# Splitting plain weight blocks by DMA: a casting transfer for the rounded half, a negative on ACT and an adding transfer for the rest

## Chip, cores and metric

The kernel runs on one core of a Trainium2 chip. Its engines are PE (matrix products; PEld is its weight load), DVE and ACT (elementwise work), POOL (a slower elementwise engine) and SP (which here only issues DMA transfers). The metric is the device time of one execution in microseconds. The kernel before took 1035.16 us in the median of three timed runs (1034.41 to 1039.77).

## What is computed

One step of a one-layer decoder on 560 tokens (16 meta tokens, 512 of a prompt, 8 x 4 of running sequences), in float32:

```python
x = x + 0.5 * swiglu(rmsnorm(x, g_ff1), w_ff1_gate, w_ff1_up, w_ff1_down)
mix, new_state = mixer(rmsnorm(x, g_mix), W, l, st)   # 4 mLSTM heads beside an RG-LRU
x = x + mix
x = x + 0.5 * swiglu(rmsnorm(x, g_ff2), w_ff2_gate, w_ff2_up, w_ff2_down)
y = rmsnorm(x, g_final)

def swiglu(x, w_gate, w_up, w_down):
    return (jax.nn.silu(x @ w_gate) * (x @ w_up)) @ w_down
```

The model width is 1024 (8 blocks of 128 rows), that of the FFNs 2816 (22 blocks). The mixer multiplies its input by `w_in` (queries, keys, values, gates, RG-LRU inputs), runs the recurrences, and multiplies the result by `w_out`.

## The kernel before

**Products.** PE multiplies operands in the type fp32r, a rounded float32. To keep float32's accuracy every operand is split into a rounded half `hi` (a copy into an fp32r tile) and a rest `lo` (the operand minus `hi`, again fp32r), and each product is made in three passes: `w_hi * x_hi`, `w_hi * x_lo`, `w_lo * x_hi` (`split_mm`, line 286).

**Weights.** They come as a list, `units`, of blocks of 128 x 512 in the order of their use. There are two kinds. *Plain* units are blocks of a weight matrix as it stands: 64 of `w_down`, 50 of `w_in`, 24 of gate and up, 16 of `w_out`, 154 in all. The others belong to 45 *sets of seven products* (Strassen's, in Winograd's form, `product7`, line 397): a set loads four quarters (`w11`, `w21`, `w22`, `w12`) and DVE makes four sums of them (`quarter_sum`, line 236), and seven units are used.

Whenever a product takes its unit (`next_w`), `run_ahead` brings four steps forward, each by its own lead in units, `AHEAD = 8, 6, 5, 4`:

- `load`: SP issues a DMA from HBM into a tile `raw` (line 223 for a plain unit, 226 for a quarter);
- `sums`: the sums of quarters, on DVE (line 236);
- `split_hi`: ACT copies `raw` (or a sum) into the fp32r tile `whi` (line 256);
- `split_lo`: DVE subtracts `whi` from `raw` and writes `wlo` (line 261).

The three kinds of tile have six buffers each (`wp`, `bufs=6`, tags `raw`, `hi`, `lo`). A load waits until the tile that it takes over is free: a `raw` is free when ACT and DVE have read it, a `whi` or `wlo` when PE has.

**Stages.** FFN 1 (from 0 to about 375 us) begins with plain units, while DVE and ACT normalise x, then alternates sets of seven products with plain units of `w_down`. The mixer (about 375 to 690 us) uses the 50 plain units of `w_in` and the 16 of `w_out`. FFN 2 (690 to about 1000 us) is built as FFN 1, and the last norm ends the kernel.

**Order.** On PE, ACT and DVE the program's own order of writing holds (tables such as `PLAN` and `FF1`). POOL and SP are placed by a scheduler. POOL's work before the change: the sums of squares of the norms (`square`, line 366, seven adds of which the last is DVE's; in FFN 1 `start_add`, line 665), the mixer's constants (lines 794 to 834, among them the masked RG-LRU weights `wrg`, `wrgh`, `wrgl`), for the gates' product `pgate` two casts that pack `lo` columns beside `hi` columns (line 873; PE uses them at 876), copies of keys and values that PE transposes, and sums for denominators. `mean` (line 379) is the product `psn` that takes `acc`, the finished sum of squares, to the mean; the scale made from it (line 383) is needed by every result of the mixer's first products.

Of the kernel before, what the change touches and what calls it, by code (L numbers as in the profile page):

```python
# [11 lines left out]
P = 128  # L12
KD = 8            # 1024 / 128
KF = 22           # 2816 / 128
T = 560           # 16 meta + 512 prompt + 8 x 4 sample tokens
C16 = 16
TQ = T - C16      # tokens whose outputs are needed
NP = 528
Q = 280           # half of the tokens
AHEAD = 8, 6, 5, 4          # how far loads, sums and both steps of the split run ahead of the products  # L20
MANUAL = {mybir.EngineType.PE, mybir.EngineType.Activation, mybir.EngineType.DVE}
TCUT = 272        # where the last row blocks are cut
DED = 7           # row blocks of h with a place of their own
PLAIN = 4, 3      # row blocks of h from plain products, in both FFNs
FT = 15           # where the last row blocks of h are cut for w_down
TAIL = 5          # row blocks of x that FFN 2 ends with
# [5 lines left out]
# the mixer, in the order of its steps (see there)  # L32
# [35 lines left out]
IN = [t for t in PLAN if t == "g" or t[0] in "kqvoxy" and t[1].isdigit()]       # row blocks of w_in  # L68
OUT = (4, 5, 6, 7, 0, 1, 2, 3)                                   # rows of w_out
# [5 lines left out]
# the beginnings of both FFNs, in the order of their steps (see `ffn`)  # L75
# [10 lines left out]
# columns of the constant array  # L86
G1, GM, G2, GF = 0, 8, 16, 24
CW = 32           # [ct, 4]
# [6 lines left out]
CS = 72           # [ct, b, 3]  # L95
H0 = 168          # [ct, b]
N0 = 200          # [h, b]
NCONST = 232

# Products of h with w_down (see `ffn`): of its second part, and under them the first part is made in quarters,  # L100
# with their sums; then the seven products of every pair of row blocks, and between them some of the others.
# [15 lines left out]
# The seven products: weights, right side, bank, and whether they open it. After one, what its bank holds goes  # L117
# into a quarter of the result.
# [6 lines left out]
# packed columns of the causal weights of one head, by block of keys  # L125
WO = (0, 512, 912, 1184, 1328, 1344)
WTOT = 1376
T0 = (16, 128, 256, 384, 512)      # first query of each block of keys
KROWS = (128, 128, 128, 128, 16, 32)

# columns of the output array of small states
# [5 lines left out]
def hymba_step(ctx, tc, xT, wgu1, wdn1, win, wout, wgu2, wdn2, consts, small, c0t, wrg,  # L137
# [6 lines left out]
    wp = ctx.enter_context(tc.tile_pool(name="wp", bufs=6))  # L144
# [4 lines left out]
    # ---------------------------------------------------------------- weights  # L149
    # Products take their weights in the order of this list, 512 columns at a time: blocks of w, or  # L150
    # quarters and sums of quarters of [gate, up] (see ups7). Loads and splits run ahead of them.
# [19 lines left out]
    def blocks(ff):  # L171
        """Row blocks of h: the plain ones, those that go through w_down by seven products, the others, and these
        in two parts."""
        a, b = PLAIN[ff], PLAIN[ff] + 8
        return (0, a), (a, b), {"d": (b, KF), "e": (b, FT), "t": (FT, KF)}
# [29 lines left out]
    loaded, ready = {}, {}  # L205
    state = {"use": 0}

    def raw_tile():
        return wp.tile([P, 512], F32, tag="raw", name="raw")

    def hl_tile():
        return (wp.tile([P, 512], F32R, tag="hi", name="whi"), wp.tile([P, 512], F32R, tag="lo", name="wlo"))
# [6 lines left out]
    def load(i):  # L219
        kind, src = units[i]  # L220
        if not kind:
            loaded[i] = raw_tile()
            nc.sync.dma_start(loaded[i][:, :src.shape[-1]], src)
        for k in {"11": ("11",), "s2": ("21", "22"), "12": ("12",)}.get(kind, ()):
            t = raw_tile()
            nc.sync.dma_start(t, src[k])
            src[k] = t

    def quarter_sum(q, k):
        """s1 = w21 + w22, s2 = s1 - w11, s3 = w11 - w21, s4 = w12 - s2, the last in place of s2."""  # L230
# [7 lines left out]
    def sums(i):  # L238
# [3 lines left out]
        b = units[i - 1 - AHEAD[1] + AHEAD[3]]           # s2 is split by now  # L242
# [6 lines left out]
    def source(i):  # L249
        kind, q = units[i]  # L250
        return q[kind] if kind else loaded[i][:, :q.shape[-1]]

    def split_hi(i):
        ready[i] = hl_tile()
        src = source(i)
        act.copy(ready[i][0][:, :src.shape[-1]], src)  # L256

    def split_lo(i):
        src = source(i)
        hi, lo = (t[:, :src.shape[-1]] for t in ready[i])  # L260
        dve.tensor_tensor(lo, src, hi, op=ALU.subtract)  # L261
# [13 lines left out]
    def split_mm(ps, ks, xh, xl, c0, first=True, last=True, hfs=(0, 1), w=None):  # L275
        """ps += w.T @ x[k] over the k of ks, in three passes of split operands."""
# [22 lines left out]
    # -------------------------------------------------------------- constants  # L299
# [16 lines left out]
    def newton(r, v, t, c=0.0):  # L316
        """One Newton step of r towards 1/sqrt(v + c)."""
# [4 lines left out]
    def rsqrt(r, v, t):  # L322
        """r = 1/sqrt(v + eps): the table's value and a Newton step."""
# [9 lines left out]
    def ars(_=0):  # L333
        """Loads the table of 1/sqrt before it is needed."""
        act.activation(dum, eps_c, AF.Abs_reciprocal_sqrt, bias=eps_c, scale=0.0)

    class Norm:
        """Splits x*g for the products and gathers the mean square beside them."""
# [49 lines left out]
    # -------------------------------------------------------------------- FFN  # L388
    # Seven products (Strassen's, in Winograd's form) of quarters of weights x quarters of a right side
    # (halves of its rows x halves of the tokens), for two row blocks of the result at a time. The last two  # L390
    # products of a pair lie behind the first of the next.
# [12 lines left out]
    def ups7(fs, c0, zs, h, xs):  # L404
        """Row blocks of silu(gate) * up: as they are where zs has a place for them, else split into h."""
# [50 lines left out]
    def down7(c0, xs):  # L456
        """Steps of the products for row blocks d and d + 4 of what the first part of h adds to x."""
# [19 lines left out]
    def h_tiles(hp, a, b, x0):  # L477
        """Tiles of h from a to b: where x was, from slot x0, and then in this pool."""
# [16 lines left out]
    def ffn(ff, nrm, c0, hp, plan, mid, steps):  # L495
        """The first row blocks come from plain products, of x * g, and go through w_down at once; under them
        the normalised x is made in quarters (halves of the rows, halves of the tokens), with the sums of
        quarters that the seven products take. down(c, h): the products of the other chunks with w_down."""
# [106 lines left out]
    # ------------------------------------------------------- FFN 1, from DRAM  # L605
# [55 lines left out]
    def start_add(d):         # on two engines: 0 to 4, 5 to 7, and both  # L661
# [5 lines left out]
    def start_warm():         # nothing reads it: the clock of the products wakes up  # L667
# [7 lines left out]
    with tc.tile_pool(name="hp1", bufs=1) as hp, tc.tile_pool(name="sp1", bufs=1) as sp:  # L675
# [9 lines left out]
        def lru_consts():  # L685
            """softplus(-lambda) = max(-lambda, 0) + log1p(exp(-|lambda|)), and halves of what goes into tanh."""
# [12 lines left out]
    # ------------------------------------------------------------------ mixer  # L699
# [4 lines left out]
    # ------------------------------------------------- FFN 2 and the last norm  # L704
    with tc.tile_pool(name="hp2", bufs=1) as hp, tc.tile_pool(name="sp2", bufs=1) as sp:
# [4 lines left out]
        def out_square(d, a, b):  # L710
            """Squares of the tokens from a to b; x becomes x*g."""
# [823 lines left out]
```

## Time and profile before

The profiled execution has a span of 1033.8 us, from its first to its last instruction; the page gives no other time of it, and the median of the timed runs is 1035.16 us.

| | |
|---|---|
| timed runs | 1035.16 us median, 1034.41 to 1039.77 |
| profiled execution, span | 1033.8 us |
| mean granted clock of TensorE | 0.989 |
| DMA instructions of SP and of POOL (from the program) | 389 and 0 |
| moved by DMA | 99.6 MB, a mean of 96 GB/s |

"Busy" is the time in which an engine had an instruction in work. Rows of groups give line, engine, operation and tiles, the number of instructions, their busy time and mean, then the idle time before them with what ended it. In DMA rows the three numbers with strokes are ns: shortest, median and longest. A bracket at the end of a row of the timeline is the wait before that instruction and what ended it. Shares in the chain of waits are of the span.

### The profile page before, as it was taken

The page shows a single profiled execution, that of the slowest core. Times are in us where ns is not written, and L with a number is a line of the kernel's source. Part 1 is how long each engine was busy: PE and PEld are TensorE (multiplying, and loading weights), DVE is VectorE, ACT ScalarE, POOL GpSimd, SP SyncE. Part 2 cuts the span into 40 slices and gives each one's busy share as a digit, 9 for nine tenths or more (in the row PEclk, how much of TensorE's full clock was granted, in tenths as well). Part 3 has the DMA queues.
Part 4 walks back from the last instruction along what each step waited for, and adds up shares of the span by engine and source line. Part 5 has one row for each costly group of instructions (what it writes and reads, how often), then busy time and mean ns, then how long its engine had stood idle before and what let it go on. Part 6 is the DMA issues. An engine that isn't in the chain of part 4 may idle for free.

```text
span 1033.8 us, 20127 instructions
## 1 busy us (share of the span) xinstructions
PE 1012.8 (98%) x7782; PEld 996.4 (96%) x7782; DVE 834.7 (81%) x1448; ACT 559.9 (54%) x1070; POOL 124.0 (12%) x185
## 2 busy tenths in 40 slices
PE   7999999999999999999999999999999999999995
PEld 7999999999999999989999999999999999999995
DVE  7889888888778797888868775789888889859774
ACT  5544555566554455466756643554555566644542
POOL 2000000000000034444443101100000000000114
PEclk9999999999999999999999999999999999999998
DMA  6322322322332334223132123122332323233222
GB/s 215 103 83 72 110 86 101 104 93 96 101 100 64 92 109 143 86 79 127 48 120 85 62 92 119 58 67 101 103 103 95 110 93 112 92 102 93 82 65 87
DMA packets 57479, 99.57 MB, mean 96 GB/s; under 512 B 7840, under 2 KB 14624, under 8 KB 57384
## 3 DMA queue, kind: packets, MB, share of 16 engines
q1 hardware_dynamic: 57384, 98.30, 29.1%
q8 instruction: 61, 1.00, 0.4%
q14 instruction: 34, 0.28, 0.1%
HBM read 93.57 MB, written 4.70 MB: 95 GB/s over the span
## 4 chain that ended last, share of the span: by engine, by line
PE 86%; DVE 7%; issue 2%; ACT 1%; POOL 1%; DMA 1%; SPq 0%; POOLq 0%; DVEq 0%; ACTq 0%
PE pb L397 26%; PE pad L397 20%; PE pd L286 15%; PE po L286 7%; PE pu L286 4%; PE pg L286 4%; PE pv L286 2%; PE py L286 2%; DVE wlo L261 1%; PE pn L1328 1%; PE pd L753 1%; PE p L286 1%; PE px L286 1%; PE pk L286 1%; PE pn L1324 0%
## 5 line engine op out<-in xcount | busy, mean ns | idle before, releaser
L256 ACT CAST whi<-raw 128x512 fp32r<-128x512 f32 (+2 forms) x289 | 173.6, 608 | 176.0 <-PE pad L397 41.1
L261 DVE TENSOR_TENSOR wlo<-raw,whi 128x512 fp32r<-128x512 f32 (+2 forms) x289 | 197.1, 699 | 69.3 <-ACT whi L256 68.9
L256 ACT CAST whi<-s 128x512 fp32r<-128x512 f32 x180 | 112.1, 623 | 105.8 <-PE pb L397 36.4
L261 DVE TENSOR_TENSOR wlo<-s,whi 128x512 fp32r<-128x512 f32 x180 | 124.2, 691 | 12.8 <-ACT whi L256 6.5
L397 PE MATMUL pad<-q21h,whi 128*128 128x280 f32 (+1 forms) x360 | 104.2, 289 | 0.9 <-ACT whi L256 0.9
L397 PE MATMUL pb<-qt4l,whi 128*128 128x280 f32 (+1 forms) x360 | 104.0, 289 | 0.0
L397 PE MATMUL pad<-q21l,whi 128*128 128x280 f32 (+1 forms) x360 | 104.0, 289 | 0.0
L397 PE MATMUL pad<-q21h,wlo 128*128 128x280 f32 (+1 forms) x360 | 104.0, 289 | 0.0
L397 PE MATMUL pb<-qt4h,whi 128*128 128x280 f32 (+1 forms) x360 | 103.9, 289 | 0.0
L397 PE MATMUL pb<-qt4h,wlo 128*128 128x280 f32 (+1 forms) x360 | 103.9, 289 | 0.0
L366 POOL TENSOR_TENSOR acc<-acc,sq 128x560 f32<-128x560 f32 (+1 forms) x12 | 18.1, 1512 | 435.1 <-ACT sq L365 434.8
L397 PEld LDWEIGHTS pad<-q21h,whi 128*128 128x128 f32 x360 | 67.8, 188 | 1.1 <-ACT whi L256 1.1
L397 PEld LDWEIGHTS pb<-qt4h,whi 128*128 128x128 f32 x360 | 67.9, 189 | 0.0
L397 PEld LDWEIGHTS pb<-qt4h,wlo 128*128 128x128 f32 x360 | 67.8, 188 | 0.0
L397 PEld LDWEIGHTS pad<-q21l,whi 128*128 128x128 f32 x360 | 67.8, 188 | 0.0
L397 PEld LDWEIGHTS pb<-qt4l,whi 128*128 128x128 f32 x360 | 67.8, 188 | 0.0
L397 PEld LDWEIGHTS pad<-q21h,wlo 128*128 128x128 f32 x360 | 67.8, 188 | 0.0
L236 DVE TENSOR_TENSOR s<-raw 128x512 f32<-128x512 f32 x90 | 61.5, 683 | 1.7 <-DMA raw<-in_wdn 1.7
L286 PE MATMUL pd<-hl,whi 128*128 128x280 f32 (+1 forms) x294 | 61.6, 291 | 0.8 <-DVE hl L529 0.8
L286 PE MATMUL pd<-hh,whi 128*128 128x280 f32 (+1 forms) x294 | 61.3, 290 | 0.8 <-ACT hh L526 0.8
L286 PE MATMUL pd<-hh,wlo 128*128 128x280 f32 (+1 forms) x294 | 61.3, 289 | 0.0
L721 POOL TENSOR_TENSOR acc<-acc,sq 128x272 f32<-128x272 f32 x12 | 11.4, 969 | 350.4 <-ACT sq L717 350.4
(457 smaller groups left out, 3029.0 us busy)
## 6 DMA issues: line engine op xcount, KB each, us to landing
raw<-in_wgu SPq DMA_DIRECT2D x174, 256.0 KB, 2.7
raw<-in_wdn SPq DMA_DIRECT2D x71, 256.0 KB, 2.8
raw<-in_win SPq DMA_DIRECT2D x50, 256.0 KB, 2.8
raw<-in_wout SPq DMA_DIRECT2D x16, 256.0 KB, 2.7
raw<-in_wdn SPq DMA_DIRECT2D x18, 192.0 KB, 2.4
out_y<-X SPq DMA_DIRECT2D x4, 544.0 KB, 3.1
c<-in_c0t SPq DMA_DIRECT2D x4, 512.0 KB, 3.6
out_o_cs<-c SPq DMA_DIRECT2D x4, 512.0 KB, 3.9
```

The lines of the kernel that those rows point to most:

```text
L236: dve.tensor_tensor(q[k], q[x], q[y], op=op)
L256: act.copy(ready[i][0][:, :src.shape[-1]], src)
L261: dve.tensor_tensor(lo, src, hi, op=ALU.subtract)
L286: state["mm"] = pe.matmul(ps[:, hf, :n], a[:, ws], b[k][:, c0 + hf * n:c0 + hf * n + n], start=first and j == 0 and i == 0, stop=last and ...
L366: (dve if d == KD - 1 else pool).tensor_tensor(self.acc[:, c0:], self.acc[:, c0:], s[:, c0:], op=ALU.add)
L397: pe.matmul(ps, a[:, k * P:k * P + P], b, start=first and k == 0 and i == 0, stop=k == KD // 2 - 1 and i == 2, skip_group_check=not first)
L721: pool.tensor_tensor(acc[:, a:b], acc[:, a:b], s[:, :b - a], op=ALU.add)
L753: pe.matmul(ps, u[:, i % 4 * P:i % 4 * P + P], v[:, C16 + a:C16 + b], start=i == 0 and m == 0, stop=f == c1 - 1 and m == 2)
L1328: pe.matmul(pn[:, 0, a:512], V[:KROWS[i], i, :P], W[:KROWS[i], WO[i]:WO[i] + 512 - a], start=i == 0, stop=i == 4)
```

## The change

For plain units alone, all three steps are made another way.

- `load`: POOL issues a DMA that reads the block from HBM as float32 and writes it as fp32r, straight into `whi` (line 223). There is no `raw` tile.
- `split_hi`: ACT writes `-whi` into `wlo` (line 258).
- `split_lo`: POOL issues a second DMA that reads the block from HBM once more and adds it to `wlo` (line 266), so that `wlo = w - whi`.

Units of the seven products keep SP's loads, ACT's copies and DVE's subtractions, but all three kinds of tile now share one tag with 18 buffers, and loads run 7 units ahead, not 8. The rest of the diff takes out comments; lines behind them move by five.

```diff
-AHEAD = 8, 6, 5, 4
+AHEAD = 7, 6, 5, 4
...
-    wp = ctx.enter_context(tc.tile_pool(name="wp", bufs=6))
+    wp = ctx.enter_context(tc.tile_pool(name="wp", bufs=18))
...
     def raw_tile():
-        return wp.tile([P, 512], F32, tag="raw", name="raw")
+        return wp.tile([P, 512], F32, tag="w", name="raw")
 
     def hl_tile():
-        return (wp.tile([P, 512], F32R, tag="hi", name="whi"), wp.tile([P, 512], F32R, tag="lo", name="wlo"))
+        return tuple(wp.tile([P, 512], F32R, tag="w", name="w" + s) for s in ("hi", "lo"))
...
         if not kind:
-            loaded[i] = raw_tile()
-            nc.sync.dma_start(loaded[i][:, :src.shape[-1]], src)
+            ready[i] = hl_tile()
+            pool.dma_start(ready[i][0][:, :src.shape[-1]], src)
...
-    def source(i):
+    def split_hi(i):
         kind, q = units[i]
-        return q[kind] if kind else loaded[i][:, :q.shape[-1]]
-
-    def split_hi(i):
-        ready[i] = hl_tile()
-        src = source(i)
-        act.copy(ready[i][0][:, :src.shape[-1]], src)
+        if kind:
+            ready[i] = hl_tile()
+            act.copy(ready[i][0], q[kind])
+        else:
+            hi, lo = (t[:, :q.shape[-1]] for t in ready[i])
+            act.mul(lo, hi.bitcast(F32), -1.0)
 
     def split_lo(i):
-        src = source(i)
-        hi, lo = (t[:, :src.shape[-1]] for t in ready[i])
-        dve.tensor_tensor(lo, src, hi, op=ALU.subtract)
+        kind, q = units[i]
+        hi, lo = ready[i]
+        if kind:
+            dve.tensor_tensor(lo, q[kind], hi, op=ALU.subtract)
+        else:
+            pool.dma_start(lo[:, :q.shape[-1]], q, accum_op=ALU.add)
```

By the built programs SP's DMA instructions fall from 389 to 235, and POOL's rise from 0 to 308. The scheduler puts them among POOL's other work. In the rows below a row is line, operation, target and sources, size and how often it repeats.

At the start of the program, before: behind POOL's four adds of squares for the first norm (`acc<-acc,sq`, line 665) come at once the adds for the mixer's norm and its gates' casts (`whi<-wlo`) and constants.

```order
L665 ISA
L665 TENSOR_TENSOR acc<-acc,sq 128x560 x4
L366 TENSOR_TENSOR acc<-acc,sq 128x560 x5
L873 CAST whi<-wlo 128x4x40 x2
L366 TENSOR_TENSOR acc<-acc,sq 128x560
L794 MEMSET ident 128x128
```

The same place in the change: `whi<-in_wgu` is a casting transfer of a block of gate or up, `wlo<-in_wgu` the adding one.

```order
L670 ISA
L670 TENSOR_TENSOR acc<-acc,sq 128x560 x4
L223 DMA whi<-in_wgu 128x512 x8
L266 DMA wlo<-in_wgu 128x512 x5
L223 DMA whi<-in_wgu 128x512
L266 DMA wlo<-in_wgu 128x512
```

The first eight casting transfers stand behind the four adds, and the first adding one behind these eight.

At the mixer's head, in the change, POOL's order from the first of the six adds for the mixer's norm (L371 now, L366 before) to the casts of the gates' block (L878 now, L873 before); the first of the six stands right ahead of these rows.

```order
L266 DMA wlo<-in_wdn 128x512
L223 DMA whi<-in_win 128x512
L266 DMA wlo<-in_wdn 128x384
L371 TENSOR_TENSOR acc<-acc,sq 128x560
L223 DMA whi<-in_win 128x512
L266 DMA wlo<-in_win 128x512
L371 TENSOR_TENSOR acc<-acc,sq 128x560
L223 DMA whi<-in_win 128x512
L266 DMA wlo<-in_win 128x512
L371 TENSOR_TENSOR acc<-acc,sq 128x560
L223 DMA whi<-in_win 128x512 x2
```

Then follow six of the mixer's constants, the fifth add, more transfers and constants, and the end of the piece:

```order
L223 DMA whi<-in_win 128x512
L266 DMA wlo<-in_win 128x512
L371 TENSOR_TENSOR acc<-acc,sq 128x560
L838 CAST wrgh_5054<-wrg 128x512
L223 DMA whi<-in_win 128x512
L266 DMA wlo<-in_win 128x512
L878 CAST whi<-wlo 128x4x40 x2
```

Between the first and the sixth add there are 15 transfers now, 7 casting and 8 adding, and the constants from `ident` (line 799 now) to `keep` (line 823); before, the constants stood behind all six adds.

On SP, the loads of quarters within a stretch of sets, with the semaphores that each waits for (DMAHW: an earlier transfer has landed; DVE, PE: that engine has gone on far enough). Before:

```order
L226 DMA raw<-in_wgu 128x512 [waits DMAHW4_49,DVE_49]
L226 DMA raw<-in_wgu 128x512 [waits DMAHW6_49,DVE_49]
L226 DMA raw<-in_wgu 128x512 [waits DMAHW7_49]
L226 DMA raw<-in_wgu 128x512 [waits DMAHW1_49,DVE_49]
L226 DMA raw<-in_wgu 128x512 [waits DMAHW0_49,DVE_49]
```

In the change:

```order
L226 DMA raw<-in_wgu 128x512 [waits DMAHW3_49,PE_49]
L226 DMA raw<-in_wgu 128x512 [waits PE_49]
L226 DMA raw<-in_wgu 128x512 [waits DMAHW5_49,DVE_49,PE_49]
L226 DMA raw<-in_wgu 128x512 [waits DMAHW6_49,DMAHW0_49,DVE_49]
L226 DMA raw<-in_wgu 128x512 [waits DMAHW7_49,PE_49]
```

A `raw` tile took over an older `raw` before, so its load waited for DVE alone; now it takes over any tile of the shared pool, and most loads wait for PE, which reads `whi` and `wlo`.

More of the change, by code (lines that the diff above doesn't have):

```diff
@@ L204, in hymba_step @@
         down_units(wdn2, d, FT, KF)
-    loaded, ready = {}, {}
+    ready = {}
     state = {"use": 0}
     def raw_tile():
-        return wp.tile([P, 512], F32, tag="raw", name="raw")
+        return wp.tile([P, 512], F32, tag="w", name="raw")
     def hl_tile():
-        return (wp.tile([P, 512], F32R, tag="hi", name="whi"), wp.tile([P, 512], F32R, tag="lo", name="wlo"))
+        return tuple(wp.tile([P, 512], F32R, tag="w", name="w" + s) for s in ("hi", "lo"))
     def w_split(t, src, c, n, copy):
```

## The prediction

> **What bounds the kernel now.** I read the head of the page first, then the windows that cut the span into the kernel's stages (columns: length, busy time of PE, PEld, DVE, ACT and POOL with the number of instructions, granted clock, share of the DMA engines, GB/s), and then the waits of PE.
>
> ```profile
> span 1033.8 us, 20127 instructions
> PE 1012.8 (98%) x7782; PEld 996.4 (96%) x7782; DVE 834.7 (81%) x1448; ACT 559.9 (54%) x1070; POOL 124.0 (12%) x185
> PE 86%; DVE 7%; issue 2%; ACT 1%; POOL 1%; DMA 1%; SPq 0%; POOLq 0%; DVEq 0%; ACTq 0%
> ...
> 0.00:25.00 25.00, 19.43 (x115) 17.94 (x116) 19.06 (x28) 14.69 (x23) 6.40 (x13) 0.93 0.64 211
> 25.00:375.00 350.00, 349.75 (x2714) 349.12 (x2714) 289.60 (x541) 182.07 (x344) 0.15 (x1) 1.00 0.29 94
> 375.00:400.00 25.00, 24.14 (x185) 23.76 (x184) 22.17 (x30) 14.61 (x25) 19.59 (x33) 1.00 0.49 161
> 400.00:550.00 150.00, 148.73 (x1081) 139.79 (x1080) 123.73 (x194) 94.73 (x196) 63.52 (x108) 0.98 0.26 86
> 550.00:690.00 140.00, 139.32 (x1073) 135.69 (x1072) 102.61 (x158) 73.59 (x130) 17.62 (x16) 0.99 0.26 85
> 690.00:1000.00 310.00, 308.70 (x2456) 308.21 (x2455) 261.27 (x475) 168.29 (x328) 3.69 (x4) 1.00 0.30 97
> ```
>
> PE is the bound. Between 25 and 1000 us it is idle for 0.25 + 0.86 + 1.27 + 0.68 + 1.30 = 4.4 us in all. The stretch from 25 to 375 us runs 2714 matmuls in 350 us, 0.129 us each, so a plain unit (24 matmuls of up to 280 columns) takes PE 3.1 us and one of the seven products (12 matmuls) 1.55 us. DVE at 81% is the busiest of the others, but almost nothing that it does is waited for. Whatever the change takes from DVE can therefore win 4.4 us at most. POOL matters in one place only: from 375 to 550 us it works 83 of 175 us, and PE's order there depends on it.
>
> **The change, part by part.** What it removes and what it puts in:
>
> ```profile
> L256 ACT CAST whi<-raw 128x512 fp32r<-128x512 f32 (+2 forms) x289 | 173.6, 608 | 176.0 <-PE pad L397 41.1
> L261 DVE TENSOR_TENSOR wlo<-raw,whi 128x512 fp32r<-128x512 f32 (+2 forms) x289 | 197.1, 699 | 69.3 <-ACT whi L256 68.9
> ...
> L223 SPq DMA_DIRECT2D raw<-in_wdn x64: 327/328/1195, 41.5 to 997.2; - x64
> L223 SPq DMA_DIRECT2D raw<-in_win x50: 327/328/669, 370.2 to 561.9; - x50
> L223 SPq DMA_DIRECT2D raw<-in_wgu x24: 327/328/978, 10.4 to 656.4; - x24
> L223 SPq DMA_DIRECT2D raw<-in_wout x16: 327/328/1542, 568.7 to 620.0; - x16
> ...
> DMA to landing us min/median/max: 2.0/2.7/4.6
> ```
>
> The plain units are the 64 + 50 + 24 + 16 = 154 loads of L223. Each loses one load on SP and one subtraction on DVE (154 x 0.70 = 108 us of DVE). ACT keeps one operation each, 0.61 us, the same size (a scaled copy in place of a cast): nothing won or lost there. POOL gets two DMA issues each, 308 in all. The DVE time and the 154 SP issues lie beside PE's work, so I give them half of the 4.4 us idle, **-2 us** (ends 0 and -4.4).
>
> **What one issue costs POOL** is the number everything hangs on, and no row shows a DMA issued by POOL. Call it c. Nearest rows: SP's issue takes 0.33 us (above), and POOL's own passes over a weight block are these:
>
> ```profile
> 392.12 0.52 POOL L829 MEMSET wrg<- 128x512 f32 x1
> ...
> 396.92 0.61 POOL L833 CAST wrgh<-wrg 128x512 fp32r<-128x512 f32 x1 [0.27 <-DMA wrg<-in_wrg]
> 397.62 1.83 POOL L834 TENSOR_TENSOR wrgl<-wrg,wrgh 128x512 fp32r<-128x512 f32 x1
> ```
>
> An issue that reads two streams should stand nearer to the two-input pass than to the cast, and the casting one nearer to the cast; I take 1.1 us for both, between 0.61 and 1.83, and keep 0.33 and 1.83 as ends. For the landing I take what SP's loads show after their issue, 2.7 - 0.33 = 2.4 us; a longer one for the accumulating transfer is covered by the lead of four units (4 x 3.1 = 12 us) everywhere but at the start. The Trainium skill (DMA: Bandwidth & Descriptors, section "SWDGE vs HWDGE vs iDMA") says that casting and accumulating transfers can be issued from GpSimd alone, which computes their descriptors in software, and puts the first byte at about 1 us against 0.6 us for the hardware path; by an estimate from that page c would be near 1 us and the sum two or three us smaller; no trace here shows it yet.
>
> **Start.** POOL's four adds of squares end at 13.13 + 1.38 = 14.5 us, then come eight casting issues, and only then the first accumulating one:
>
> ```profile
> 13.13 1.38 POOL L665 TENSOR_TENSOR acc<-acc,sq 128x560 f32<-128x560 f32 x1 [0.79 <-ACT sq L659]
> ...
> 26.66 0.42 PE L286 MATMUL pg<-xh,wlo 128*128 128x280 f32 x2
> ```
>
> The first rest lands at 14.5 + 9 x 1.1 + 2.4 = 26.8 us; PE asks for it at 26.66. **+0.2 us** (0 at c = 0.33, +6.7 at 1.83). The next ones come every 1.1 us, while PE takes 3.1 us for each.
>
> **The sum of squares at the mixer's head.** In the kernel before, POOL does seven things in a row here; columns are start, length, operation and the wait before it.
>
> ```profile
> 374.85 1.77 POOL L366 TENSOR_TENSOR acc<-acc,sq 128x560 f32<-128x560 f32 x1 [360.33 <-ACT sq L365]
> 377.89 6.90 POOL L366 TENSOR_TENSOR acc<-acc,sq 128x560 f32<-128x560 f32 x4 [1.27 <-ACT sq L365]
> 387.01 1.44 POOL L873 CAST whi<-wlo 128x160 fp32r<-128x160 f32 x2 [2.23 <-DVE wlo L261]
> 388.85 1.46 POOL L366 TENSOR_TENSOR acc<-acc,sq 128x560 f32<-128x560 f32 x1 [0.40 <-ACT sq L365]
> 390.25 0.20 POOL L794 MEMSET ident<- 128x128 f32 x1
> ...
> 395.97 0.69 POOL L813 TENSOR_SCALAR_AFFINE_SELECT seqm<-seqm 32x8 f32<-32x8 f32 x3
> ...
> 393.83 0.74 DVE L366 TENSOR_TENSOR acc<-acc,sq 128x560 f32<-128x560 f32 x1
> ...
> 395.42 1.10 PE L379 MATMUL psn<-acc,ones 128*128 128x280 f32 x4
> 396.15 0.63 PE L876 MATMUL pgate<-xh,whi 128*128 128x280 f32 x2
> ```
>
> The six adds ended at 390.3 us, five before PE's `psn` at 395.42, which needs them. In the new order 15 DMA issues and nearly all of the mixer's constants (390.25 to about 395.6) stand between the first add and the last. From the first add's start: 374.85 + 6 x 1.44 + 5.3 + 15c = 388.8 + 15c; with DVE's own last add (0.8 with its hand-over) `psn` can start at 389.6 + 15c, so PE waits 15c - 5.8 us: **+10.7** at 1.1 (0 below c = 0.39, +21.6 at 1.83). Right behind it `pgate` needs L878's two casts of the gates' block: between the last add and them stand a cast (0.61) and two issues, then 1.44 of their own. That is 2.05 + 2c after the last add, and PE gets there 0.8 + 0.73 after it: 0.5 + 2c, **+2.7** (+1.2 to +4.2).
>
> **The rest of the mixer's first half.**
>
> ```profile
> raw<-in_win SPq DMA_DIRECT2D x32, 256.0 KB, 2.8
> ```
>
> This is the DMA view from 400 to 550 us: 32 plain loads, hence 64 issues. POOL's load becomes 63.5 + 64 x 1.1 = 133.9 of 150 us, 89%, in an order that may not be left: the copies of keys and values that PE transposes, the masked weights and the denominators' sums of four heads queue behind two or three issues each. Ends: 0, where the slack of these 12 hand-overs holds, and at c = 1.83 an overload of 63.5 + 117.1 - 150 = 31 us. I take a third of 12 x 2.2, **+8**. From 550 to 690 us POOL has 17.6 us of its own and 42 loads: 110 of 140 us, with little that PE waits for; nothing.
>
> **The quarters of the seven products.** They keep their path through SP, but share one pool of 18 tiles with everything, and loads run 7 units ahead in place of 8, while their sums stay at 6.
>
> ```profile
> L226 SPq DMA_DIRECT2D raw<-in_wgu x148: 327/328/1414, 59.5 to 887.0; - x148
> ...
> DMA to landing us min/median/max: 2.5/2.7/4.7
> ```
>
> The lead of a load over its sum falls from two products to one, 3.1 to 1.55 us, and the load waits for PE to give a tile back, no longer for DVE. A pair lands 2.7 + 0.4 after its issue. DVE will wait in some of the 45 sets; what reaches PE is between 0 and 45 x 0.6 (one landing of 2.7 less 1.55, halved by PE's own slack) = 27 us. Most landings are near the shortest (2.5 against 2.7 in the middle): **+4**.
>
> **Sum at c = 1.1:** 0.2 + 10.7 + 2.7 + 8 + 4 - 2 = +23.6, so 1033.8 becomes a span of 1057.4. The median of the timed runs, 1035.16, lies 1.4 above the profiled span: **1059 us**.
>
> **Rivals.**
> 1. *POOL's issue is short (c about 0.33, like SP's).* For it: the issue moves no data. Then `psn` waits for nothing, `pgate` 1.2, the half mixer 63.5 + 21 of 150 us for nothing, quarters up to 4, less 2: 1035 to 1038, not slower. It decides at c = 0.39, where 15c passes 5.8 us. Against it: POOL's smallest pass over a block takes 0.52 us. Chance 0.15.
> 2. *The accumulating issue or transfer costs double (c = 1.1 and 2.2).* It reads its target too. Of the 15 issues 8 are accumulating: 7.7 + 17.6 - 5.8 = 19.5; start 14.5 + 8.8 + 2.2 + 2.4 - 26.7 = 1.2; `pgate` 3.8; the half mixer 63.5 + 32 x 3.3 = 169 of 150, 19 + 8; quarters 4, less 2; plain stretches of the FFNs 3.3 against 3.1 us a unit, 50 x 0.2 = 10: +64, 1099 us. Chance 0.17.
> 3. *POOL's issues and DVE get in each other's way.*
>
> ```profile
> 8.03 4.31 POOL L665 TENSOR_TENSOR acc<-acc,sq 128x560 f32<-128x560 f32 x3 [6.57 <-ACT sq L659]
> 3.98 0.29 DVE L636 CAST whi<-raw 128x256 fp32r<-128x256 f32 x1 [3.98 <-DMA raw<-in_wgu]
> 8.52 2.52 DVE L636 CAST whi<-raw 128x256 fp32r<-128x256 f32 x2 [0.53 <-DMA raw<-in_wgu]
> ```
>
> Beside POOL's adds a cast of 0.29 us takes 1.26. If issues did the same to DVE at half that strength, DVE in 375 to 550 us (146 us, less 43 x 0.7 = 30) would grow by half of 95 us, to 163 of 175 with PE waiting on its hand-overs: some +15 more, 1074. The Trainium skill (SBUF — State Buffer, section "Who interferes with whom") says that a two-input DVE instruction contends with GpSimd instructions that read SBUF, not with those that only write, and infers that descriptor generation writes; by that rule this rival adds nothing. The adds here read, so the row agrees with the rule as far as it goes. Chance 0.05.
> 4. *The quarters are late in most sets:* +23 more, 1082. Chance 0.05.
>
> That the transfer might not round (rests of zero) would leave the time as it is, since all steps would still run; it is no case of its own.
>
> **How the numbers follow.** The forecast, POOL late in the mixer's first half with c from about 0.7 to 1.5, has 0.58. The range takes in the upper part of rival 1 and reaches past rival 2 to c near 1.6 for all issues: 1036 to 1115. 0.5% of 1035, about what a measurement of this kernel can tell from no change, is 5.2 us. Faster by more would need over the whole idle time of PE (4.4 us): 0.02. Within it: rival 1 less that, 0.13. Slower: 0.85.
>
> **What would show it.** POOL's DMA rows give c outright. PE's waits should name POOL (`psn` behind `acc`, `pgate` behind the gates' cast) near 395 to 415 us, about 13 us together; the windows should show PE full before 375 and after 690 us, POOL near 90% from 375 to 550, DVE near 730 us busy. I am wrong if c is under 0.4, if the stall is in the FFNs' plain stretches (then transfers are the cause), or if `s` at L236 waits for `raw` in most sets.

## The result and the profile after

The changed kernel takes 1051.09 us in the median of four runs (1046.68 to 1053.82), the kernel before 1035.84 beside it: a ratio of 1.0129, 95% interval 1.0106 to 1.0153. It is slower, as forecast, by 15 us and not by 24. The profiled execution has a span of 1047.9 us, 14.1 more than that of before.

The head of the page and the windows of the changed kernel, with the columns of the prediction:

```profile
span 1047.9 us, 20184 instructions
PE 1014.3 (97%) x7782; PEld 999.0 (95%) x7782; DVE 742.7 (71%) x1294; ACT 540.0 (52%) x1070; POOL 334.2 (32%) x493
PE 83%; POOL 5%; DVE 4%; DMA 3%; issue 2%; ACT 1%; SPq 1%; POOLq 0%; DVEq 0%; ACTq 0%
...
25.00:375.00 350.00, 347.93 (x2695) 346.79 (x2694) 264.70 (x500) 170.38 (x341) 52.71 (x74) 1.00 0.46 119
375.00:400.00 25.00, 22.54 (x172) 21.96 (x171) 16.10 (x20) 13.86 (x24) 22.70 (x40) 1.00 0.88 203
400.00:550.00 150.00, 140.75 (x1016) 134.38 (x1017) 99.27 (x153) 85.12 (x175) 103.07 (x172) 0.97 0.71 152
550.00:690.00 140.00, 139.52 (x1077) 136.04 (x1076) 79.17 (x116) 78.90 (x146) 81.18 (x110) 1.00 0.74 155
```

DVE lost 92 us of its work (834.7 - 742.7; 108 had been forecast), and PE is still the bound. The largest part of the loss is where POOL works most, from 375 to 550 us, where PE is idle for 2.5 + 9.3 us. POOL is busy for 22.7 + 103.1 of these 175 us, 72% and not near 90%. PE's waits in the same trace (total us, times, longest):

```profile
PE prg L1054 <- POOL wrgl L839: 3.4, 1, 3.4
PE psn L384 <- DVE acc L371: 3.1, 1, 3.1
PE pt L1204 <- DVE xp L1026: 2.8, 1, 2.8
...
PE pv L291 <- DVE xl L360: 2.4, 1, 2.4
PE pb L402 <- ACT t L446: 1.8, 2, 1.4
```

In the kernel before, PE did not wait at `psn` and `pt`, nor at `pv` for `xl`. Its longest wait between 25 and 1000 us, and that at `prg`, were these:

```profile
PE pad L397 <- ACT whi L256: 0.9, 1, 0.9
...
PE prg L1049 <- POOL wrgl L834: 0.3, 1, 0.3
```

PE runs the same 7782 matmuls in both kernels, and in the same order but for 81 of them near 1000 us, so the start of one and the same matmul in both traces tells how far the change is behind at that point:

```
place                              before    after     behind
start (first row block)             19.52    19.71      0.2
seven products of FFN 1            190.66   193.22      2.6
the last of them                   381.51   383.06      1.6
mixer, pv                          392.31   396.72      4.4
psn                                395.42   403.07      7.7
within pgate                       398.94   408.45      9.5
within prg                         441.48   454.22     12.7
before pt                          459.52   470.57     11.1
behind pt                          478.24   493.45     15.2
end of the mixer's first half      579.64   590.79     11.2
last matmul of the kernel         1023.88  1036.43     12.6
```

### The profile page after: what moved, and what is told of

The parts are those of the page before. It is cut to its first block, busy times and chain, and to the rows that moved or that the text cites. A ratio compares the mean times of both kernels' runs of the same rounds, so it can differ in the third digit from the quotient of the medians.

```text
span 1047.9 us, 20184 instructions
## 1 busy us (share of the span) xinstructions
PE 1014.3 (97%) x7782; PEld 999.0 (95%) x7782; DVE 742.7 (71%) x1294; ACT 540.0 (52%) x1070; POOL 334.2 (32%) x493
## 3 DMA queue, kind: packets, MB, share of 16 engines
q0 software_dynamic: 44352, 76.57, 36.1%
q1 hardware_dynamic: 35208, 60.01, 17.7%
## 4 chain that ended last, share of the span: by engine, by line
PE 83%; POOL 5%; DVE 4%; DMA 3%; issue 2%; ACT 1%; SPq 1%; POOLq 0%; DVEq 0%; ACTq 0%
PE pb L402 25%; PE pad L402 19%; PE pd L291 14%; PE po L291 6%; PE pg L291 4%; PE pu L291 4%; PE py L291 2%; PE pq L291 1%; PE pk L291 1%; DMA raw<-in_wgu 1%; PE px L291 1%; PE pd L758 1%; PE p L291 1%; POOL whi L223 1%; POOL wlo L266 1%
## 5 line engine op out<-in xcount | busy, mean ns | idle before, releaser
L223 POOL DMA_DIRECT2D whi<-in_wdn x64 | 48.3, 814 | 504.6 <-DVE wlo L264 406.0
L255 ACT CAST whi<-s 128x512 fp32r<-128x512 f32 x180 | 106.0, 620 | 43.8 <-DVE s L236 28.7
L258 ACT ACTIVATE wlo<-whi 128x512 fp32r<-128x512 f32 (+1 forms) x154 | 88.0, 602 | 60.9 <-DMA whi<-in_wdn 17.1
L264 DVE TENSOR_TENSOR wlo<-raw,whi 128x512 fp32r<-128x512 f32 x135 | 93.0, 690 | 25.7 <-ACT whi L255 21.2
L236 DVE TENSOR_TENSOR s<-raw 128x512 f32<-128x512 f32 x90 | 62.4, 693 | 40.5 <-DMA raw<-in_wgu 34.3
L255 ACT CAST whi<-raw 128x512 fp32r<-128x512 f32 x135 | 76.3, 616 | 21.8 <-PE pad L402 7.5
L266 POOL DMA_DIRECT2D wlo<-in_wdn x64 | 60.5, 1067 | 61.6 <-ACT wlo L258 51.5
L444 ACT ACTIVATE t<-t 128x272 f32<-128x272 f32 (+1 forms) x37 | 16.1, 435 | 95.3 <-DVE t L421 95.3
```

The costliest lines, as they stand in the source:

```text
L223: pool.dma_start(ready[i][0][:, :src.shape[-1]], src)
L236: dve.tensor_tensor(q[k], q[x], q[y], op=op)
L255: act.copy(ready[i][0], q[kind])
L258: act.mul(lo, hi.bitcast(F32), -1.0)
L264: dve.tensor_tensor(lo, q[kind], hi, op=ALU.subtract)
L266: pool.dma_start(lo[:, :q.shape[-1]], q, accum_op=ALU.add)
```

## The experiments

Two theories stood against each other. *POOL's order*: an engine takes its instructions one after the other, and what PE needs of POOL stands behind transfers there. *Transfers*: twice the reading from HBM, and landings of 5 to 6 us, make weights or other loads late. A third, *shared tiles*, blames the one tag of 18 buffers and the lead of 7. None of the kernels leaves anything of the computation out.

**Halves of the change.** By the flag `by_dma(i)` a plain unit goes the new way or the old one, in the shared tiles:

```diff
+    def by_dma(i):
+        return not first_mix <= i < last_mix      # e2: first_mix <= i < last_mix
...
-        if not kind:
+        if not kind and not by_dma(i):
+            loaded[i] = raw_tile()
+            nc.sync.dma_start(loaded[i][:, :src.shape[-1]], src)
+        elif not kind:
             ready[i] = hl_tile()
```

> Plain units of the FFNs by the new way, those of w_in and w_out (66 of 154) by the old one, in the same shared pool. Theory 'POOL's order' (the time is lost where the norm's adds, the gates' casts, wrgl and the transposed copies queue behind POOL's transfers between 375 and 500 us): most of the 11 us that PE loses there goes, what stays is 2 to 4 us at the seven products and at most 3 us at the mixer's head, where transfers of w_down still stand among the adds: 1036 to 1043 us. Rival 'transfers' (38 MB more from HBM, and landings of 5 to 6 us): the loss goes with the number of transfers, 88/154 of 15 us is left: 1044 us. Rival 'shared tiles and lead 7': nothing changes, 1050 us.

> The other half: w_in and w_out by the new way, both FFNs by the old one, same shared pool. 'POOL's order': the mixer keeps its loss of 8 to 11 us, the seven products 2 to 4 us: 1045 to 1051 us. 'Transfers': 66/154 of 15 us, 1042 us. 'Shared tiles and lead 7': 1050 us. The two first runs together should give the loss of the whole change, with the seven products' part counted twice.

With the new way in the FFNs alone: 1040.56 us, ratio 1.0043 (1.0026 to 1.0060). With it in the mixer alone: 1052.0 us, 1.0154 (1.0123 to 1.0186). In the first, PE is 2.8 us behind the kernel before at the end of FFN 1 and 0.2 at 500 us; in the second, it is 3.5 us behind at the end of FFN 1 and 12.7 at the end of the mixer's first half. Together they lose 4.4 + 15.9 = 20.3 us where the whole change loses 15.3; the seven products lose in both. Not the number of transfers decides (88 units by the new way cost 4 us, 66 cost 16), but where they stand. And in the second, the seven products of FFN 1 have no transfer of POOL's beside them, and PE falls from 0.9 us ahead to 3.5 behind there all the same.

**The norm's adds off POOL.**

```diff
-(dve if d == KD - 1 else pool).tensor_tensor(self.acc[:, c0:], ...
+(dve if d == KD - 1 or self.g == GM else pool).tensor_tensor(self.acc[:, c0:], ...
```

> The whole change, but the six adds of squares for the mixer's norm run on DVE and not on POOL (6 x 0.74 us on DVE, which has 9 us idle from 375 to 400 us). 'POOL's order': psn waits for POOL no longer; the 6 us that PE lost up to psn go but for 1 to 2, and the gates' casts come earlier too: 1043 to 1047 us. 'Transfers' and 'shared tiles': 1050 us, as the change.

1045.6 us, 1.0094 (1.0064 to 1.0124). `psn` starts without a wait, PE is 2.3 us behind at 425 us and not 9.5. But the next wait grew:

```profile
PE prg L1054 <- POOL wrgl L839: 5.0, 1, 5.0
```

**Half of POOL's transfers, the same bytes read.**

```diff
             pool.dma_start(ready[i][0][:, :src.shape[-1]], src)
+            loaded[i] = raw_tile()
+            nc.sync.dma_start(loaded[i][:, :src.shape[-1]], src)
...
-            act.mul(lo, hi.bitcast(F32), -1.0)
...
-            pool.dma_start(lo[:, :q.shape[-1]], q, accum_op=ALU.add)
+            dve.tensor_tensor(lo, loaded[i][:, :q.shape[-1]], hi, op=ALU.subtract)
```

> The rounded half of plain units by POOL's casting transfer, but the rest made as before: SP loads the block once more as raw, and DVE subtracts (154 x 0.69 us on DVE again). Bytes read from HBM are those of the change, POOL's issues are half (154). Each plain unit holds three tiles of the shared pool, not two. 'POOL's order': the loss in the mixer is halved or better: 1037 to 1045 us. 'Transfers': the same bytes, 1048 to 1052 us. 'Shared tiles': more tiles are held, 1050 us or more.

1047.26 us, 1.0097 (1.0059 to 1.0134): between both expectations. `psn` waits no longer, and the mixer's first half loses 6.7 us (from 4.3 behind to 11.0) where the change loses 9.6; but PE loses 5.5 us at the seven products of both FFNs (3.8 in the change), where three tiles of a plain unit and not two now stand in the shared pool; the expectation had left that out.

**The shared tiles alone, the lead, and both.** The kernel before with the change's pool; the change with quarters 8 ahead again; the kernel before with a lead of 7 and its own tags:

```diff
-AHEAD = 8, 6, 5, 4          (e5 and e12)
+AHEAD = 7, 6, 5, 4
-    wp = ctx.enter_context(tc.tile_pool(name="wp", bufs=6))      (e5, with one tag "w" for raw, hi, lo)
+    wp = ctx.enter_context(tc.tile_pool(name="wp", bufs=18))
...
-        for fn, n in zip((load, sums, split_hi, split_lo), AHEAD):      (e8)
+        for fn, n in zip((load_q, load, sums, split_hi, split_lo), (8, *AHEAD)):
```

> The kernel before, with its own loads, casts and subtractions, but with one tag of 18 tiles for raw, hi and lo and loads 7 units ahead, as in the change. No transfer of POOL's. If the loss at the seven products (some 2.5 us in FFN 1 and 1.5 in FFN 2) is made by the shared tiles and the lead of 7: PE loses 3 to 5 us there and nothing in the mixer, 1038 to 1042 us. If it is made by POOL's transfers beside the loads of quarters: 1036 us, as before.

> The change, with quarters of the seven products loaded 8 units ahead again and plain units 7, all in the shared 18 tiles. If the lead is what costs at the seven products, their 4 us go and DVE's 40 us of waits for raw shrink to some 10: 1045 to 1048 us. If it is the shared tiles, whose reuse makes a load wait for PE: no change, 1049 to 1052 us.

> The kernel before, its own tags of six tiles each, but loads 7 units ahead and not 8. If the lead alone makes DVE wait for quarters: 35 of 45 sets wait for raw as in the change, some 40 us on DVE, and PE loses 3 to 9 us at the seven products: 1038 to 1045 us. If the lead only costs where the tiles are shared (as a load then also waits for PE): a few us of DVE's waits and 1035 to 1037 us.

In this order, they took 1044.75 us, 1.0091 (1.0072 to 1.0109); 1048.89 us, 1.0134 (1.0108 to 1.0160); 1037.22 us, 1.0008 (0.9993 to 1.0022). How long DVE's sums of quarters wait for `raw` (us, times), in the changed kernel:

```profile
  DMA raw<-in_wgu: 34.3, 33
  DMA raw<-in_wdn: 6.2, 2
```

In the kernel with the shared tiles alone, which has no transfer of POOL's:

```profile
  DMA raw<-in_wgu: 38.6, 33
  DMA raw<-in_wdn: 2.5, 2
```

And with the lead of 7 in tiles of their own:

```profile
  DMA raw<-in_wdn: 1.9, 1
```

In the change with 8 ahead it is 4.9 us in 4 places. So the waits in 35 of 45 sets come with the shared tiles *and* the lead of 7 together, and POOL's transfers have no part in them; either one without the other has hardly any.

The kernel with the shared tiles alone missed its expectation: it lost 9.5 us, not 3 to 5. In its trace PE falls back by 4.3 us in FFN 1 and by 2.4 in FFN 2, and by another 2.6 in the mixer, where nothing was expected and where PE is idle for 0.8 us in all: there its granted clock was lower (third number from the right, 0.95; 0.98 in the kernel before; more on this in the next section):

```profile
400.00:550.00 150.00, 149.18 (x1057) 139.53 (x1056) 121.14 (x188) 91.63 (x186) 62.31 (x105) 0.95 0.30 91
```

So the shared tiles and the lead cost the FFNs 6.7 us there and 3.8 in the change. The change leaves DVE more free time, which may be the reason; no run shows it.

In the change with 8 ahead PE loses 0.4 us at the seven products of FFN 1 and not 2.4. Its time as a whole can't be told from the change's: the two intervals overlap, and in its profiled execution PE lost some 6 us more than in the change's between 408 and 600 us, in the mixer, which this edit doesn't touch.

**The bytes without POOL's order.** SP reads each plain block a second time, into a scratch:

```diff
+            nc.sync.dma_start(dr.tile([P, 512], F32, tag="again", name="again")[:, :src.shape[-1]], src)
```

> The kernel before, in which SP reads every plain block a second time, into a scratch in HBM that nothing uses: 38 MB more read, as in the change, and the same bytes written once more, but POOL's order is that of before. 'POOL's order' alone: 1036 to 1038 us. If the slower landing of small transfers in the mixer (wrg 6 us after its issue and not 2.4, Wb 6.6 and not 3.7) is a cause of its own: wrg and Wb land late here too, prg waits for wrgl by 2 to 4 us near 441 us, and the mixer loses 3 to 6 us: 1039 to 1043 us.

1081.37 us, 1.0442 (1.0422 to 1.0461), and no answer to the question. Nothing depends on the second reads, so the scheduler put those of nearly all later matrices between 59 and 157 us, ahead of quarters that PE needed:

```profile
85.01 14.88 SPq L225 DMA_DIRECT2D again<-in_win  x19
100.38 0.82 SPq L228 DMA_DIRECT2D raw<-in_wgu  x2
```

PE falls 45 us behind there and nowhere else. In the mixer this kernel had no second reads, so it doesn't test the transfers; it shows on SP what the change meets on POOL: what stands in front in a queue holds what stands behind.

**The RG-LRU's weights earlier.** With the adds on DVE as well:

```diff
-k0 gc
+k0 rg0 gc
-k1 gf L0 eq0 ex0 cx0 gp hq0 hk0 ek1 rg0 gq hx0 tv0
+k1 gf L0 eq0 ex0 cx0 gp hq0 hk0 ek1 gq hx0 tv0
```

> The change with the six adds on DVE, as in the run before, and with the second group of the RG-LRU's weights (wrg: its memset, load, cast and subtraction) brought forward by one line of the mixer's plan, some 10 us. If prg's wait of 5 us comes from wrg's late load in POOL's queue, it goes: 1039 to 1042 us, 5 us under the run with the adds alone. If the mixer's stalls only move to the next thing that POOL owes (the transposed copies, the denominators), 1044 to 1046 us.

1043.92 us, 1.0088 (1.0068 to 1.0107). The wait of `prg` is gone, as said, and the time is nearly that of the rival: the stalls moved on, to

```profile
PE pt L1204 <- DVE xp L1026: 3.1, 1, 3.1
...
PE pq L291 <- DVE kT L864: 2.4, 1, 2.4
```

**Everything that PE waited for off POOL**, then the same with quarters 8 ahead:

```diff
-        pool.tensor_copy(wh, t)
-        pool.tensor_tensor(wl, t, wh.bitcast(F32), op=ALU.subtract)
+    def do_rh(g):                       # in PLAN: q1 rh0 rh1 a0 ...
+        act.copy(wh, t)
+        dve.tensor_tensor(wl, t, wh.bitcast(F32), op=ALU.subtract)
...
-                pool.tensor_copy(hv[:, :, 64:104], lv[:, :, 0:40].bitcast(F32))
+                dve.tensor_copy(hv[:, :, 64:104], lv[:, :, 0:40].bitcast(F32))
...
-        pool.tensor_tensor(tr, tr, a0, op=ALU.mult)
+        dve.tensor_tensor(tr, tr, a0, op=ALU.mult)
```

> The change, with everything that PE was seen to wait for in POOL's queue made elsewhere: the six adds, the gates' casts and the RG-LRU's product th with its two small fills on DVE, the RG-LRU weights' cast on ACT and their subtraction on DVE, just ahead of their use. POOL keeps the transfers, the constants and what nobody waited for. 'POOL's order': the stalls at psn, pgate, prg and the one behind th go, 8 to 10 of the mixer's 11 us, and only the seven products' 4 us stay: 1038 to 1042 us. If the slow landing of the change's transfers is what holds the mixer, or the stalls move on to what POOL still owes: 1045 to 1048 us.

> The same with quarters loaded 8 units ahead. If the lead is worth what the look at positions said in the run with it alone (1.6 us in FFN 1, 1.0 in FFN 2), 2 to 3 us less than the run before: 1036 to 1039 us; faster than the kernel before only if the 4.4 us of PE's idle time there shrink too.

1032.92 us, 0.9966 (0.9948 to 0.9984), and 1029.96 us, 0.9933 (0.9913 to 0.9953): better than I had expected of either theory, and faster than the kernel before. The windows of the second:

```profile
375.00:400.00 25.00, 25.00 (x192) 24.74 (x191) 19.91 (x34) 14.85 (x26) 19.44 (x42) 1.00 1.07 253
400.00:550.00 150.00, 150.00 (x1102) 143.12 (x1101) 112.47 (x174) 97.65 (x207) 101.33 (x166) 0.98 0.70 153
```

PE is idle for nothing from 375 to 550 us, although the transfers are all there (DMA engines busy for 70%, 153 GB/s, as in the change), and POOL is nearly as busy as in the change (120.8 of 175 us, and 125.8). So neither the bytes nor POOL's load cost time by themselves.

**The control: the same moves in the kernel before.**

> The control: the kernel before, with the same work moved from POOL to DVE and ACT as in the run e9, and nothing of the change. If the gain of e10 (0.9933) comes from the DVE time that the change frees, this one stays at the kernel before or behind it, 1035 to 1038 us: DVE is at 81% here and gets some 10 us more between 375 and 550 us. If moving the work is itself the gain, whatever the weights' path: 1030 to 1033 us.

1032.95 us, 0.9965 (0.9951 to 0.9979). Without the change, moving the work is already a gain of 3.6 us. With these moves the change costs nothing and gains nothing (1032.92 beside 1032.95), and with 8 ahead it stands 3.0 us lower (1029.96); the intervals of these two ratios, 0.9913 to 0.9953 and 0.9951 to 0.9979, still touch, so that a gain from the change itself is not shown.

## Why the prediction was right in kind and too large

**One issue's cost, c, was mis-sized: 0.57 us, not 1.1.** From the timeline of the change (start, length):

```profile
14.78 4.45 POOL L223 DMA_DIRECT2D whi<-in_wgu  x8
...
418.64 2.66 POOL L266 DMA_DIRECT2D wlo<-in_win  x3 [1.69 <-ACT wlo L258]
420.36 1.51 POOL L223 DMA_DIRECT2D whi<-in_win  x1
```

Eight casting issues take 4.45 us, 0.56 each; three accumulating ones hold the next instruction back for 1.72 us, 0.57 each, though a row of them is shown as longer than that. With it POOL's load from 400 to 550 us comes out: 63.5 + 64 x 0.57 = 100.0, where 133.9 had been forecast and 103.1 was measured. That is nearest to the cast of POOL's (0.61) and not to the two-input pass that I leaned on. The Trainium skill (DMA: Bandwidth & Descriptors, section "Specifications") puts the first byte of a transfer from POOL at about 1 us, from which I had made an estimate of c near 1 us; the trace decides. An accumulating issue costs POOL no more than a casting one, which ends rival 2. Rival 1 (a short issue, no loss) had its turning point at c = 0.39, and 0.57 is past it.

**The start: +0.2 forecast, 0.1 measured.** The 0.2 us of the table's first row are there before PE comes to the first blocks of POOL's; from 20 to 60 us it falls back by 0.1. With c = 0.57 the forecast's formula gives no wait here. That is not safe in every execution: in the trace of e9, with the same start, PE waited 1.8 us for an accumulating transfer.

**The sum of squares: +10.7 forecast, 6.1 measured, by another sum.** With c = 0.57 the forecast's own formula gives psn at 389.6 + 15 x 0.57 = 398.2 us, a wait of 2.8. It started at 403.07. What I had left out is that a transfer *waits* in POOL's queue, for a tile that PE must give back or for ACT's negative, and holds everything behind it. The two largest of these waits over the whole kernel and, below them, the timeline of the change at this place:

```profile
POOL wlo L266 <- ACT wlo L258: 81.3, 44, 7.7
...
POOL whi L223 <- PE pd L291: 41.9, 10, 8.8
```

```profile
375.54 0.67 ACT L370 ACTIVATE sq<-X 128x560 f32<-128x560 f32 x1
...
376.58 0.53 POOL L223 DMA_DIRECT2D whi<-in_win  x1 [1.03 <-PE pb L402]
377.12 1.41 POOL L371 TENSOR_TENSOR acc<-acc,sq 128x560 f32<-128x560 f32 x1
...
390.98 0.20 POOL L799 MEMSET ident<- 128x128 f32 x1 [1.08 <-PE pd L291]
...
392.46 3.58 DVE L360 SCALAR_TENSOR_TENSOR xl<-X,C,xh 128x560 fp32r<-128x560 f32 x2
...
397.52 0.80 DVE L360 SCALAR_TENSOR_TENSOR xl<-X,C,xh 128x560 fp32r<-128x560 f32 x1 [0.83 <-ACT xh L359]
...
400.51 1.36 POOL L371 TENSOR_TENSOR acc<-acc,sq 128x560 f32<-128x560 f32 x1
401.90 1.11 DVE L371 TENSOR_TENSOR acc<-acc,sq 128x560 f32<-128x560 f32 x1 [3.58 <-POOL acc L371]
```

The first add starts 2.3 us later than before: ACT has its square ready only at 376.2 us, 1.4 after the first add's start in the kernel before, and then a casting transfer that had waited for a tile of PE's stands ahead of it. The sixth add ends 24.7 us after the first's start, of which six adds are 8.2 and 15 issues 8.6; the formula has 22.5 for this, and half of the difference is POOL's wait for PE of 1.1 us at `ident`. DVE's last add and its hand-over take 1.2 us and not 0.8. These three make up the 4.9 us, of which POOL's own waits are some 2. And 2.8 of the 6.1 us arise before `psn`, at `pv`: the fifth add now runs at 394 us, beside two of DVE's passes for `xl` that `pv` needs, and these take 3.58 us, where one takes 0.80 by itself. The run e3 shows the place to be right: without these adds on POOL both are gone. Too high a price and missing waits partly made up for each other; that the term came within 5 us is in part luck.

**The gates' casts: +2.7 forecast, 1.8 measured, and the cause was wrong.** `pgate` never waited for POOL; PE is slower there. Windows of the change, with the granted clock third from the right, and two rows of PE around the wait at `prg`:

```profile
403.00:406.00 3.00, 2.93 (x13) 2.44 (x14) 1.57 (x5) 2.00 (x4) 2.85 (x8) 0.77 0.89 160
406.00:409.00 3.00, 3.00 (x18) 3.00 (x18) 2.83 (x4) 0.63 (x1) 2.93 (x5) 0.66 0.34 57
409.00:412.00 3.00, 3.00 (x25) 3.00 (x25) 1.76 (x4) 0.63 (x1) 3.00 (x6) 1.00 0.94 221
...
490.00:494.00 4.00, 3.41 (x18) 3.36 (x19) 3.21 (x7) 2.80 (x9) 2.05 (x7) 0.58 0.45 122
```

```profile
448.93 0.30 PE L1054 MATMUL prg<-xcl,wrgh 128*128 128x292 f32 x1
...
453.25 0.45 PE L1054 MATMUL prg<-xcl,wrgh 128*128 128x292 f32 x1
```

Behind each of the three waits of some 3 us (at `psn`, `prg` and `pt`) PE runs its next matmuls at a lower clock, 0.58 to 0.77 in the windows at `psn` and `pt`, which costs 1 to 2 us more; behind the wait of 2.4 us at `pv` it does not (1.00 from 396 to 403 us). The Trainium skill (TensorE: Matmul & The Clock Gate, section "Part 1: The HAM clock gate") says that the clock falls to half after an idle window of about 3.4 us; here it was down after waits of 3.1 and 2.8 us, and in the kernel before without any wait, as shown below.

**The rest of the mixer's first half: +8 forecast, 3.2 at prg and 4.1 at pt measured.** (A third of 12 x 2.2 is 8.8.) Two hand-overs were late, not a part of all twelve. The second as the timeline shows it:

```profile
479.50 1.16 POOL L223 DMA_DIRECT2D whi<-in_win  x2
480.64 1.86 POOL L266 DMA_DIRECT2D wlo<-in_win  x2
481.75 1.32 POOL L223 DMA_DIRECT2D whi<-in_win  x1
482.28 2.57 POOL L266 DMA_DIRECT2D wlo<-in_win  x2
484.32 1.09 POOL L223 DMA_DIRECT2D whi<-in_win  x1
...
486.94 1.80 POOL L1087 TENSOR_TENSOR th<-th,a 128x584 f32<-128x584 f32 x1
488.78 0.46 DVE L1089 TENSOR_SCALAR a<-a 128x584 f32<-128x584 f32 x1 [5.90 <-POOL th L1087]
...
490.26 0.18 DVE L1026 TENSOR_TENSOR xp<-px,r 128x32 f32<-128x32 f32 x1
...
490.59 1.09 PE L1204 MATMUL pt<-ident,kT 128*128 128x128 f32 x4 [2.82 <-DVE xp L1026]
```

DVE stands for 5.9 us on one product of POOL's that is queued behind eight transfers and seven small operations, and PE stands on what DVE would have freed. At `prg` a slower landing has the larger share: from the end of its memset to its cast `wrg` took 6.1 us and not 3.2. Whether the weights' transfers made it late was not isolated, since e6 failed to; in e10 loads of `wrg` land 6.5 us after their issue, and PE waits for nothing.

**The quarters: +4 forecast, 3.8 measured** (2.4 in FFN 1, 1.4 in FFN 2). I had written that waits for raw in most sets would prove me wrong; they came in 35 sets, 40.5 us on DVE, and PE saw a tenth of it. Rival 4 had the wait right and its price wrong. The reason that I gave, the lead, is half of it: e12 shows that in tiles of its own a lead of 7 is enough.

**What DVE's freed time gives back: -2 forecast, -1.6 measured at most; -5.0 by the clock and +1.6 at the end that no term had.** The steps up in the table add to 0.2 + 2.4 + 2.8 + 3.3 + 1.8 + 3.2 + 4.1 + 1.4 = 19.2 us, and PE's last matmul is 12.6 behind: 6.6 us came back. Of these 1.0 is the wait for `whi` near 380 us, which is gone, and 0.6 falls in short waits near 526 us. The other 5.0 came back in three places of some 1.7 us each (the first is the step from 12.7 to 11.1), where the kernel *before* ran slow although PE waited for nothing, within the products `pn`, right behind 16 of them that have only 4 columns:

```profile
450.00:475.00 25.00, 25.00 (x171) 23.10 (x171) 21.43 (x31) 16.42 (x28) 13.08 (x18) 0.93 0.22 67
...
575.00:600.00 25.00, 25.00 (x177) 23.07 (x176) 18.16 (x30) 14.11 (x26) 1.64 (x1) 0.94 0.18 61
...
496.00:500.00 4.00, 4.00 (x10) 2.10 (x9) 4.00 (x5) 3.54 (x4) 3.56 (x3) 0.57 0.00 0
```

The change ran these products at the full clock (1.00 from 550 to 690 us in its windows above). In its timed runs the kernel before itself has a mean clock between 0.986 and 0.993, so the share of such stretches changes from one execution to the next; why one is slow in one trace and not in another, no run here shows. These 5 us nearly cancel what PE lost by the clock behind its three waits, and that is luck, not DVE's freed time. Against it, 1.6 us are lost behind the last matmul (see the last section).

**Rival 3**, issues that slow DVE, is refuted: 262 instructions of DVE in this trace overlap an issue of POOL's and no other work of POOL's, and none of them is longer by a quarter than the median of its form. What POOL's two-input passes stretch of DVE's is 27 to 29 us in both kernels, by the same count. The rule of the Trainium skill (SBUF — State Buffer, section "Who interferes with whom") that I had weighed against it agrees. The row that I had shown beside that rule, though, was a cast with one input, which the rule's words on two inputs don't cover; a two-input pass of DVE's took 1.98 us beside POOL's adds in the kernel before and 0.80 without (`xl`, at 10.96 and 6.86 us).

## What to carry to other kernels

An engine that becomes an issuer of transfers takes over their waits, for free tiles and for earlier steps, and all its other work stands behind them; before moving transfers to it, move away from it what others wait for. Where a busy engine is freed, look at who then stands on the critical path: here the 92 us taken from DVE bought nothing. When 17 us of POOL's work (334 to 317) had gone to other engines the loss was gone too, but the same moves without the change gave the same time; only with the longer lead did the change stand 3.0 us lower, and the intervals touch. A pool shared by tiles of unlike lives makes a load wait for the longest of them; give it lead, or tiles of its own.

## What the runs showed of the hardware

- This program ends later with transfers of POOL's. Behind the last matmul's start the change needs 11.5 us and the kernel before 9.9, with the same work; POOL's longest drain is 7.96 us in all six traces with 308 of its transfers, 7.35 with 176 (e1), 6.70 with 132 (e2) and 3.16 in all five without. The rows of three drains (shortest, middle and longest, ns), in the change:

```profile
L1521 POOLq DRAIN  x3: 40/102/7963, 1039.1 to 1047.6; - x3
```

and before:

```profile
L1516 POOLq DRAIN  x3: 34/78/3159, 1026.6 to 1033.6; - x3
```

- The same megabyte kept the DMA engines busy for longer when POOL had issued it: 76.57 MB took 36.1% of 16 engines' span, where SP's 60.01 MB took 17.7%, 1.6 times as much for each.
- From issue to landing the casting transfers took 4.9 us in the median and the accumulating ones 6.1, where SP's loads of the same blocks had taken 2.7. In the change's list of waits PE waits for none of them; in e9's it waits once for an accumulating one, 1.8 us.
